# First group of a Strassen-like matmul: two sums of B ahead of a transpose, and the transfers of A and B interleaved

## The chip, the cores and the metric

One core of a Trainium2 chip. The time is the device time of one execution in microseconds (us); a median is over several executions of the same kernel. The span of a trace runs from the first to the last instruction of the traced execution and is some 1.6 us shorter than its time.

## The reference, cut to what matters

```python
def reference(a, b):            # a: 4096 x 4096, b: 4096 x 4096, float32
    x = np.matmul(a, b)
    return 0.5 * x * (1 + np.tanh(np.sqrt(2 / np.pi) * (x + 0.044715 * x**3)))
```

## The kernel before

The kernel computes each 2 x 2 block with seven products M1 to M7 instead of eight, on float16 copies of A and B that the loads cast from float32. A product's operands are blocks or sums of blocks: VectorE makes the sums ("aS" of A, "bS" of B) and transposes A. TensorE adds up a product's results in accumulators called banks. A block is 512 rows and the work goes in groups. Group 0 has nothing to hide its loads behind, so its first halves (suffix `_0` below) run as plain products and the second halves (`_1`) as M3, M5, M7, M1, M4, M2, M6. What each step waits for is put in a fixed order by hand.

```python
PRODUCTS = [                                   # name, bank, operand of A, operand of B
    ("M3", "Y", "11", ("12", "22", 1)),
    ("M5", "X", ("11", "12", -1), "22"),
    ("M7", "X", ("12", "22", -1), ("21", "22", 1)),
    ("M1", "X", ("11", "22", -1), ("11", "22", -1)),
    ("M4", "X", "22", ("21", "11", 1)),
    # ... M2, M6
]

def load_a(mb, quad, c, h=None):               # A: 4 transfers of 256 KB
    # ... cut
    for g in range(4):
        nc.gpsimd.dma_start(out=s[g * Q : (g + 1) * Q, x : x + n, :],
                            in_=a_v[kh * CH + c, g, :, x0 : x0 + n, :])

def make_sums(gi, s, q):                       # the sums of one step: A's, then B's
    # ... cut
    for tiles, blk, o, tag in ((a_tiles, mb, oa, "aS"), (b_tiles, nb, ob, "bS")):
        # ... cut
        t = pool.tile([P, 4 * NC], F16, name=tag, tag=tag, bufs=AHEAD + 1)
        nc.vector.tensor_tensor(out=t[:, :], in0=part(tiles, blk, o[0], q), in1=part(tiles, blk, o[1], q),
                                op=ALU.add if o[2] > 0 else ALU.subtract)

for n, whats in (                              # before step n: loads (A, B) and transposes (T)
    (0, "A11_0 B12_0 T11_0 B11_0 A12_0 B22_0 B21_0 A21_0"),
    (4, "T12_0 A22_0"),
    (7, "T21_0"),
    (8, "B12_1 B22_1 A11_1 T22_0 A12_1 B21_1"),
    (14, "T11_1 A22_1 B11_1"),
    (16, "T12_1 A21_1"),
    (18, "T22_1"),
    (22, "T21_1"),
): ...

for n, step in enumerate(steps):               # the order that every engine's queue gets
    for fn, args in before.get(n, ()):
        fn(*args)
    if n + AHEAD < len(steps):                 # sums two steps ahead
        make_sums(*steps[n + AHEAD])           # (cut: only for steps of products)
    flush()                                    # outputs that wait: add the plain part, Gelu, store
    combine()
    plain(n) if step[1] < 0 else multiply(*step)
```

M5's results are kept by ScalarE in buffers "m5" and go into outputs y; M7's results are copied by ScalarE out of their banks into buffers "x7", and M1 then adds into the same banks.

## Time and profile before

| | kernel before |
|---|---|
| median of three executions | 1582.06 us (1581.94 to 1584.08) |
| span in the trace (that execution took 1583.98 us) | 1582.3 us |
| TensorE busy | 1570.4 us |
| M5 ends, at full pace | 85.02 us |
| A22's second half transposed from | 82.89 us |
| M1 starts | 98.33 us |

TensorE is busy for 99% of the time, so the whole question is about 6.4 us between 85 and 98. The prediction below shows the lines for it. One more view belongs to it, GpSimd's timeline, as it issues the loads (start, duration, operation, how many, idle before):

```profile
55.33 0.65 POOL L149 DMA_DIRECT2D stage<-in_a_dram  x1 [0.36 <-issue]
57.52 4.46 POOL L149 DMA_DIRECT2D stage<-in_a_dram  x7 [1.54 <-issue]
```

The first line is the first transfer of A11, the second begins 1.54 us later: GpSimd stopped, and the trace names no semaphore for it.

### The profile page before, as it was taken

The numbers are of one execution on the slowest core, as the hardware profiler recorded it, in microseconds if no ns is written. First come the engines' busy times: TensorE is split into PE (matmuls) and PEld (weight loads), VectorE is DVE, ScalarE is ACT, GpSimd is POOL, SyncE is SP. The second block draws the span as 40 slices with busy tenths as digits, with TensorE's granted clock in tenths as the row PEclk, the third lists the DMA queues.
The fourth block names the chain that finished last, engine by engine and source line by source line (L and its number), as shares of the span: only waits on it lengthen the run. The fifth ranks groups of instructions, "written<-read, shape, count | busy, mean of one in ns | idle before, by whom it ended". The sixth has DMA issues, their size and how long they took to land. (4 is left out here: it accounts for less than half of the span.)

```text
span 1582.3 us, 19668 instructions
## 1 busy us (share of the span) xinstructions
PE 1570.4 (99%) x7254; PEld 710.5 (45%) x7254; DVE 1227.5 (78%) x1371; ACT 517.6 (33%) x710; POOL 535.7 (34%) x976
## 2 busy tenths in 40 slices
PE   9989999999999999999999999999999999999998
PEld 4434444444444444444444444444444444444443
DVE  1488898867877888895778788888687778988775
ACT  0026454411121545431112354542111145364111
POOL 7663441430333144341124414245011443314400
PEclk9999999999999999999999999999999999999999
DMA  9998793891957488587496837779468885748802
GB/s 174 188 221 182 107 191 68 152 184 31 204 97 146 110 133 160 104 161 135 72 168 115 183 76 137 150 109 191 81 115 151 134 160 90 150 107 133 161 27 81
DMA packets 224982, 211.12 MB, mean 133 GB/s; under 512 B 20080, under 2 KB 192112, under 8 KB 224880
## 3 DMA queue, kind: packets, MB, share of 16 engines
q0 software_dynamic: 187584, 142.67, 61.4%
q1 hardware_dynamic: 37296, 67.13, 11.8%
q8 instruction: 59, 0.97, 0.2%
q14 instruction: 43, 0.35, 0.1%
HBM read 285.22 MB, written 67.11 MB: 223 GB/s over the span
## 5 line engine op out<-in xcount | busy, mean ns | idle before, releaser
L310 PEld LDWEIGHTS <-aS 128*128 128x128 f16 x4960 | 485.6, 98 | 591.4 <-issue 4.4
L176 POOL DMA_DIRECT2D bR<-in_b_dram x832 | 447.8, 545 | 707.7 <-DVE bS L283 340.9
L283 DVE TENSOR_TENSOR aS<-aT 128x2048 f16<-128x2048 f16 x310 | 375.8, 1218 | 151.5 <-PE accX L310 115.0
L310 PE MATMUL accX<-bS,aS 128*128 128x512 f16 x1984 | 432.7, 380 | 4.5 <-DVE bS L283 2.5
L283 DVE TENSOR_TENSOR bS<-bR 128x2048 f16<-128x2048 f16 x310 | 375.8, 1217 | 69.4 <-PE accX L310 58.5
L310 PEld LDWEIGHTS <-aT 128*128 128x128 f16 x1984 | 194.1, 98 | 234.5 <-issue 0.5
L408 ACT ACTIVATE y<-y 128x512 f32<-128x512 f32 x192 | 118.5, 630 | 352.8 <-DVE y L417 352.4
L310 PE MATMUL accY<-bS,aT 128*128 128x512 f16 x992 | 216.9, 379 | 0.3 <-DVE bS L283 0.3
L310 PE MATMUL accY<-bS,aS 128*128 128x512 f16 x992 | 216.7, 379 | 0.0
L310 PE MATMUL accX<-bR,aS 128*128 128x512 f16 x992 | 216.7, 379 | 0.0
L310 PE MATMUL accX<-bS,aT 128*128 128x512 f16 x992 | 216.7, 379 | 0.0
L310 PE MATMUL accY<-bR,aS 128*128 128x512 f16 x992 | 216.7, 379 | 0.0
L149 POOL DMA_DIRECT2D stage<-in_a_dram x140 | 87.8, 633 | 247.8 <-DVE aT L162 176.5
L417 DVE TENSOR_TENSOR energy<-energy,square 128x1024 bf16<-128x1024 bf16 x240 | 164.2, 684 | 9.5 <-ACT square L200 5.7
L381 ACT COPY x<-accX 128x512 f32<-128x512 f32 x128 | 74.6, 585 | 223.7 <-PE accX L310 223.7
L200 ACT ACTIVATE square<-aT 128x1024 bf16<-128x1024 f16 x120 | 123.4, 1050 | 70.4 <-DVE energy L417 70.0
L200 ACT ACTIVATE square<-bR 128x1024 bf16<-128x1024 f16 x120 | 123.0, 1050 | 62.4 <-DVE energy L417 60.5
L162 DVE STREAM_TRANSPOSE aT<-stage 128x2048 uint32<-128x2048 uint32 (+1 forms) x36 | 74.3, 2067 | 66.0 <-DMA stage<-in_a_dram 66.0
L381 ACT COPY m<-accX 128x512 f32<-128x512 f32 x60 | 34.8, 580 | 198.6 <-PE accX L310 192.1
L408 ACT ACTIVATE y<-accX 128x512 f32<-128x512 f32 x64 | 38.2, 597 | 100.2 <-PE accX L310 99.9
L417 DVE TENSOR_TENSOR x<-accX,x 128x512 f32<-128x512 f32 x64 | 44.0, 691 | 21.9 <-ACT y L408 19.1
L417 DVE TENSOR_TENSOR y<-accY,m 128x512 f32<-128x512 f32 x60 | 39.9, 686 | 12.5 <-ACT m L381 12.4
(40 smaller groups left out, 341.2 us busy)
## 6 DMA issues: line engine op xcount, KB each, us to landing
bR<-in_b_dram POOLq DMA_DIRECT2D x832, 128.0 KB, 5.2
out_dram<-y SPq DMA_DIRECT2D x256, 256.0 KB, 5.8
stage<-in_a_dram POOLq DMA_DIRECT2D x116, 256.0 KB, 6.8
stage<-in_a_dram POOLq DMA_DIRECT2D x24, 128.0 KB, 5.1
row<-seen_d SPq DMA_DIRECT2D x2, 1.5 KB, 3.8
seen_d<-seen SPq DMA_DIRECT2D x1, 3.0 KB, 7.1
```

Of the source, the lines that this page charges most:

```text
L149: nc.gpsimd.dma_start(out=s[g * Q : (g + 1) * Q, x : x + n, :], in_=a_v[kh * CH + c, g, :, x0 : x0 + n, :],)
L162: nc.vector.transpose(dst[:, :, x, :], src[:, :, x, :])
L176: nc.gpsimd.dma_start(out=t[g * Q : (g + 1) * Q, e::2, :], in_=b_v[kh * CH + c, g, e, :, :, n0 : n0 + NC],)
L200: nc.scalar.activation(t[:, :], src, ACT.Square)
L283: nc.vector.tensor_tensor(out=t[:, :], in0=part(tiles, blk, o[0], q), in1=part(tiles, blk, o[1], q), op=ALU.add if o[2] > 0 else ALU.subtract,
L310: nc.tensor.matmul(acc[:, :], sa[:, j // 2, i * P : (i + 1) * P, j % 2], sb[:, j, :], start=start and j == 0, stop=stop and j == 3, skip_g ...
L381: nc.scalar.copy(out=t[:, :], in_=src[:, :])
L408: nc.scalar.activation(y[:, :], src[:, :], ACT.Gelu_apprx_tanh)
L417: nc.vector.tensor_tensor(out=o[:, :], in0=x[:, :], in1=y[:, :], op=op)
```

## The change

The intent is twofold. M7's two sums of B need no transpose, so they can be made while VectorE waits for A22. And A's transfers are twice as large as B's, so interleaving them keeps more bytes in flight, as only eight transfers are ever under way (in the trace each issue waits for the landing of the eighth one back). The core of the diff:

```diff
-        for g in range(4):
-            nc.gpsimd.dma_start(out=s[...], in_=a_v[...])
+        return [(s[...], a_v[...]) for g in range(4)]
...
+    def load(*pairs):
+        lists = [fn(*args) for fn, args in pairs]
+        order = sorted(((k + 0.5) / len(ts), x, k) for x, ts in enumerate(lists) for k in range(len(ts)))
+        for _, x, k in order:
+            dst, src = lists[x][k]
+            nc.gpsimd.dma_start(out=dst, in_=src)
...
-    def make_sums(gi, s, q):
+    def make_sums(gi, s, q, only=None):        # only="bS": B's sum now, kept for the step
...
-        (8, "B12_1 B22_1 A11_1 T22_0 A12_1 B21_1"),
+        (8, "A11_1+B12_1+B22_1 T22_0 A12_1+B21_1"),
...
-        (18, "T22_1"),
+        (18, "S2 S3 T22_1"),
```

`S2 S3` are the two sums of B for M7's two steps; `+` joins loads that are interleaved. The other groups' loads go through `load` one at a time, in their old order.

More of the change, by code (lines that the diff above doesn't have):

```diff
@@ L147, in load_a @@
         s = staged[mb, quad, c]
-        for g in range(4):
-            nc.gpsimd.dma_start(
-                out=s[g * Q : (g + 1) * Q, x : x + n, :],
-                in_=a_v[kh * CH + c, g, :, x0 : x0 + n, :],
-            )
+        return [
+            (s[g * Q : (g + 1) * Q, x : x + n, :], a_v[kh * CH + c, g, :, x0 : x0 + n, :])
+            for g in range(4)
+        ]
     def turn_a(mb, quad, c, h=None):
@@ L173, in load_b @@
         t = b_tiles[nb, quad, c]
-        for e in range(2) if h is None else (h,):
-            for g in range(4):
-                nc.gpsimd.dma_start(
-                    out=t[g * Q : (g + 1) * Q, e::2, :],
-                    in_=b_v[kh * CH + c, g, e, :, :, n0 : n0 + NC],
-                )
+        return [
+            (t[g * Q : (g + 1) * Q, e::2, :], b_v[kh * CH + c, g, e, :, :, n0 : n0 + NC])
+            for e in (range(2) if h is None else (h,)) for g in range(4)
+        ]
+    def load(*pairs):
+        lists = [fn(*args) for fn, args in pairs]
+        order = sorted(
+            ((k + 0.5) / len(ts), x, k) for x, ts in enumerate(lists) for k in range(len(ts))
+        )
+        for _, x, k in order:
+            dst, src = lists[x][k]
+            nc.gpsimd.dma_start(out=dst, in_=src)
     def part(tiles, blk, quad, q):
@@ L278, in make_sums @@
         for tiles, blk, o, tag in ((a_tiles, mb, oa, "aS"), (b_tiles, nb, ob, "bS")):
+            if only not in (None, tag):
+                continue
             if isinstance(o, str):
                 got.append(part(tiles, blk, o, q))
+                continue
+            if (tag, gi, s, q) in sums:
+                got.append(sums.pop((tag, gi, s, q)))
                 continue
@@ L287, in make_sums @@
             got.append(t)
+            if tag == only:
+                sums[tag, gi, s, q] = t
+                return
         sums[gi, s, q] = got
@@ L480, in half_path @@
         for what in whats.split():
-            fn = {"A": load_a, "B": load_b, "T": turn_a}[what[0]]
-            for h in (0, 1) if what[4] == "0" and what != "A11_0" else (None,):
-                before.setdefault(n, []).append((fn, (0, what[1:3], int(what[4]), h)))
+            half = what[-1] == "0" and what != "A11_0"
+            if what[0] == "S":
+                before.setdefault(n, []).append((make_sums, (0, 2, int(what[1]), "bS")))
+                continue
+            for h in (0, 1) if half else (None,):
+                args = [(x[0], (0, x[1:3], int(x[4]), h)) for x in what.split("+")]
+                if what[0] == "T":
+                    before.setdefault(n, []).append((turn_a, args[0][1]))
+                else:
+                    pairs = [({"A": load_a, "B": load_b}[x], xs) for x, xs in args]
+                    before.setdefault(n, []).append((load, pairs))
     before[4].append((idle, (N_IDLE,)))
@@ L504, in half_path @@
                 early = gi == 0 and c == 0
-                at(gi, 3 - early, 2 * c + 1, load_b, nb1, "12", c)
-                at(gi, 4 - early, 2 * c + 1, load_b, nb1, "22", c)
-                at(gi, 6, 2 * c + 1, load_b, nb1, "21", c)
+                at(gi, 3 - early, 2 * c + 1, load, (load_b, (nb1, "12", c)))
+                at(gi, 4 - early, 2 * c + 1, load, (load_b, (nb1, "22", c)))
+                at(gi, 6, 2 * c + 1, load, (load_b, (nb1, "21", c)))
             if na:
-                at(gi, 4, c, load_a, mb1, "11", c)
+                at(gi, 4, c, load, (load_a, (mb1, "11", c)))
                 at(gi, 5, 2 * c, turn_a, mb1, "11", c)
-                at(gi, 5, 2 * c + 1, load_a, mb1, "12", c)
+                at(gi, 5, 2 * c + 1, load, (load_a, (mb1, "12", c)))
                 at(gi, 6, 2 * c, turn_a, mb1, "12", c)
-                at(gi, 6, 2 * c + 1, load_a, mb1, "22", c)
+                at(gi, 6, 2 * c + 1, load, (load_a, (mb1, "22", c)))
                 at(gi + 1, 0, 2 * c + 1, turn_a, mb1, "22", c)
-                at(gi + 1, 1, c, load_a, mb1, "21", c)
+                at(gi + 1, 1, c, load, (load_a, (mb1, "21", c)))
                 at(gi + 1, 3 + c, 0, turn_a, mb1, "21", c)
             if nbb:
-                at(gi, 6, 2 * c + 1, load_b, nb1, "11", c)
+                at(gi, 6, 2 * c + 1, load, (load_b, (nb1, "11", c)))
     for mb in range(NMB):
```

## The prediction

> **What bounds the kernel now.** First the page: the engine rows and the slices say which engine sets the end.
>
> ```profile
> span 1582.3 us, 19668 instructions
> PE 1570.4 (99%) x7254; PEld 710.5 (45%) x7254; DVE 1227.5 (78%) x1371; ACT 517.6 (33%) x710; POOL 535.7 (34%) x976
> PE   9989999999999999999999999999999999999998
> ```
>
> TensorE is idle for 1582.3 - 1570.4 = 11.9 us in all. About 1.4 us lie before the first matmul and about 5 us behind the last one (the final output), so no reordering in the first group can win more than some 6 us, 0.4% of the time. The third slice is one of the few below 9, so next I read the list of TensorE's waits:
>
> ```profile
> PE accX L310 <- DVE bS L283: 2.5, 1, 2.5
> PE accX L310 <- DVE aS L283: 1.6, 1, 1.6
> PE accX L310 <- ACT m L381: 0.4, 1, 0.4
> ```
>
> Then TensorE's own timeline around them (start, duration, operation, count, idle before):
>
> ```profile
> 87.66 3.13 PE L310 MATMUL accX<-bS,aS 128*128 128x512 f16 x8 [2.48 <-DVE bS L283]
> 91.20 5.52 PE L310 MATMUL accX<-bS,aS 128*128 128x512 f16 x24 [0.41 <-ACT m L381]
> 98.33 7.07 PE L310 MATMUL accX<-bS,aS 128*128 128x512 f16 x32 [1.62 <-DVE aS L283]
> ```
>
> The first two rows are M7 of group 0 (32 matmuls), the third is M1. M5 ended at 85.02 in issue time (78.11 + 32 x 0.216). At full pace M7 would run from 85.02 and M1 from 91.93; M1 starts at 98.33. So **6.4 us** are lost here, and M4, M2 and everything later follow from M1's start almost without a wait. The start of M1 is therefore the quantity to predict. Its cause is on VectorE, which works its queue in order:
>
> ```profile
> 82.89 2.31 DVE L162 STREAM_TRANSPOSE aT<-stage 128x2048 uint32<-128x2048 uint32 x1 [4.90 <-DMA stage<-in_a_dram]
> 85.24 1.23 DVE L283 TENSOR_TENSOR aS<-aT 128x2048 f16<-128x2048 f16 x1
> 86.38 1.22 DVE L283 TENSOR_TENSOR bS<-bR 128x2048 f16<-128x2048 f16 x1
> 87.52 1.22 DVE L283 TENSOR_TENSOR aS<-aT 128x2048 f16<-128x2048 f16 x1
> 88.65 1.22 DVE L283 TENSOR_TENSOR bS<-bR 128x2048 f16<-128x2048 f16 x1
> 89.79 2.68 DVE L417 TENSOR_TENSOR y<-accY,m 128x512 f32<-128x512 f32 x4
> 92.39 1.21 DVE L283 TENSOR_TENSOR aS<-aT 128x2048 f16<-128x2048 f16 x1
> 93.52 1.22 DVE L283 TENSOR_TENSOR bS<-bR 128x2048 f16<-128x2048 f16 x1
> 94.65 2.49 DVE L417 TENSOR_TENSOR y<-y,x 128x512 f32<-128x512 f32 x4
> 97.71 2.03 ACT L381 COPY x<-accX 128x512 f32<-128x512 f32 x4
> ```
>
> VectorE sits idle for 4.90 us until A22's second half lands, transposes it, and from there to 97 has no gap at all. The last line is ScalarE's: the copies of M7's banks, which M1 overwrites. They stand behind four Gelus, which wait for the additions at 94.65. First copy 97.71 + 0.58 = 98.29, M1 at 98.33: M1 waits for this chain, and "aS" in its wait row is only the tie that ended last by name. So M1 = start of A22's transpose (82.89) + 15.44 us of serial work.
>
> **What the Trainium skill says.** "VectorE: DVE Perf Modes", section "The perf-mode tier table": a 16-bit tensor_tensor of 2048 elements takes 1224 ns at the 2x rate. The trace agrees: 1218 ns, with 1.13 to 1.14 us from start to start. "DMA: Bandwidth & Descriptors", section "Where 436 GB/s comes from": about 358 GB/s from HBM and 435 GB/s of fabric per core. These loads cast float32 to half, so they read twice what they write; the trace's best stretches write 202 GB/s, thus read 404: between the two figures, and I take the DMA engines as the bound of the loads rather than the number of bytes in flight. "TensorE: Matmul & The Clock Gate", section "What's actually happening": activity is judged in free-running windows of 3413 ns, and an idle one halves the clock. The trace has one such window, after the 2.48 us of idle time:
>
> ```profile
> 84.00:88.00 4.00, 1.52 (x8) 0.55 (x7) 3.96 (x4) 0.08 (x1) 3.94 (x7) 1.00 1.27 188
> 88.00:92.00 4.00, 3.59 (x11) 1.16 (x9) 3.89 (x6) 1.17 (x2) 1.81 (x4) 0.57 1.43 193
> 96.00:100.00 4.00, 2.38 (x12) 0.98 (x11) 4.00 (x5) 3.74 (x8) 2.80 (x7) 1.00 1.21 230
> ```
>
> The granted clock (third number from the end) falls to 0.57 there: M7's first eight matmuls take 3.13 us instead of 1.7. After the 1.62 us of idle time it stays at 1.00. So a window need not be wholly idle to be punished, but 1.6 us of 3.4 are not enough.
>
> **The change, part 1: M7's two sums of B go in front of A22's transpose.** Nothing is added or removed; two tensor_tensors move. They need B21 and B22 only. B21 lands at about 77 in the kernel before (its eight issues start between 62 and 72 and land some 5 us after the last), so they fit in the 4.90 us where VectorE waits. Behind the transpose 2 x 1.135 = 2.27 us fall away. M1 = transpose + 15.44 - 2.27 = transpose + **13.17 us**.
>
> **Part 2: transfers woven.** In the changed order the 16 issues of B12 and B22 take A11's four in between (B B A B B ...), and B21's eight take A12's four (B A B B A B ...); A22 follows alone as before. Bytes ahead of A22 are the same. What the kernel before loses there is seen in GpSimd's issues: it stops 1.54 us between A11's first and second issue, for no semaphore that the trace names and while VectorE is idle; an issue always starts about 0.3 us after the landing of the eighth one back, so only eight transfers are in flight, and eight of B (128 KB each) are just 5.2 us of work at 0.65 us each. So a stop empties the engines:
>
> ```profile
> 52.00:56.00 4.00, 4.00 (x20) 1.86 (x19) 0.00 (x0) 1.30 (x3) 3.19 (x6) 1.00 1.24 202
> 60.00:64.00 4.00, 4.00 (x20) 1.85 (x19) 0.00 (x0) 0.00 (x0) 2.65 (x6) 1.00 1.31 168
> 72.00:76.00 4.00, 4.00 (x21) 1.81 (x19) 3.97 (x5) 0.00 (x0) 3.65 (x7) 1.00 1.15 173
> ```
>
> From the landings one by one: 2.92 us between A11's first two where 1.32 is the pace (1.6 lost), and about 0.6 lost over A22's own four, when only B's were in flight ahead of them: 2.2 us at most to be had. With A woven in, eight issues hold 1.6 of A's on average in the first stretch and 2.7 in the second, which is 6.3 and 7.0 us of work instead of 5.2. I expect the 0.6 back and 0.4 of the 1.6, as the stop stays. A22 would land at 82.8 - 1.0 = 81.8.
>
> But weaving makes **A12 later**. It landed whole at 71.67, with B21 behind it; now its last piece is the eleventh of twelve. From 48.94 (the landing before this stretch) come 24 issues of B at 0.65 and 8 of A at 1.32 = 26.2 us, so B21 is done at 75.1 without any stop and A12 at 74.5; with 1.2 us of stop, at 75.7. Its transpose started at 73.30 and now starts at about 75.8; M5 needs it plus the first difference, 2.33 + 1.2 us, thus 79.3 instead of 78.11: **a new wait of about 1.2 us before M5** (0 without any stop). VectorE then goes on: transpose 2.33, four sums at 1.135, so it comes to A22's transpose at 75.8 + 2.33 + 4.54 = **82.7**. A22 has landed by then; the order on VectorE, not the transfer, sets it.
>
> **Sum.** M1 = 82.7 + 13.2 = 95.9 instead of 98.33: 2.4 us sooner. M5's wait and M7's disappear in it: M7 starts at 82.7 + 2.33 + 1.2 = 86.2, close behind M5's end (79.3 + 6.9), waits some 0.7 us for its third bank (ScalarE's copy behind the first y), ends near 93.9, and M1 waits some 2 us for its copies. Behind M1 the order is the old one, and the later loads have slack or move with the rest. 1582.06 - 2.4 = **1579.6**.
>
> **Rivals.** (1) The stop disappears too, since more is in flight: A12 at 74.5, A22's transpose at 81.4, M1 at 94.6, time 1578.3. For it: the deeper stock of work; against: GpSimd issues nothing in that time whatever the order. (2) The wait moves to A12: if it lands at 77, M5 waits 2.5 us, VectorE comes to A22's transpose at 84, M1 at 97, and 1581 remain. For it: M5's margin before was 1.3 us only (its first difference done at 76.8, used at 78.11). (3) The idle time before M1 (1.6 us before, about 2 now) may fall into one clock window and cost up to 1.7 us at half rate on the very chain that sets the end: 1581.3. For it: 2.48 us did it; against: 1.62 did not. One chance in four; where the window lies differs between executions, which may also be why the three runs before spread over 2.1 us. (4) The full 6.4 us come back: 1575.7; against it stands the chain of y, Gelu and copies, which the change leaves.
>
> **Range and chances.** Rivals 1 and 2, with about 0.5 us of spread between runs, give 1577.6 to 1581.6. A 2% step is 31.6 us, five times all that TensorE loses in this place; nothing that the change touches could add that much either, as the instructions are the same. Faster by over 2%: 0.004; within 2%: 0.99; slower: 0.006.
>
> **What would show it.** In VectorE's timeline: two bS between the second aS of M5 and A22's transpose, the transpose at 82 to 83 with little or no idle time before it, M1 some 13.2 us later. In TensorE's: a new wait of 0 to 1.5 us before M5 (near 78), under 0.5 before M7, about 2 before M1. In the rates: no stretch near 170 GB/s around A22's issues. It is wrong if A22's transpose still waits for its transfer, if M1 follows the transpose by 15 us, if the half clock falls on M1, or if the gain is lost later to a wait for outputs in group 1.

## The result, and the profile after

| | before | changed |
|---|---|---|
| median of six executions | 1582.88 us (1581.94 to 1584.08) | 1580.62 us (1579.66 to 1581.45) |
| ratio | | 0.9985 (95%: 0.9972 to 0.9998) |
| span in the trace | 1582.3 | 1578.4 |
| A22's transpose | 82.89 | 81.35 |
| M1 starts | 98.33 | 94.52 |

A ratio is from runs of both kernels in the same rounds; it isn't quite the ratio of the medians or of the means. The gain is 2.3 us by medians, where 2.4 were forecast, and 1580.62 lies in the range.

TensorE's timeline of the changed kernel in the same place (M7 in two rows, then M1):

```profile
85.34 1.89 PE L325 MATMUL accX<-bS,aS 128*128 128x512 f16 x8
87.39 5.34 PE L325 MATMUL accX<-bS,aS 128*128 128x512 f16 x24 [0.16 <-ACT m L396]
94.52 7.07 PE L325 MATMUL accX<-bS,aS 128*128 128x512 f16 x32 [1.79 <-ACT x L396]
```

The wait before M7 is gone, the one before M1 has stayed (1.79 us against 1.62) and in this trace carries the name of ScalarE's copy, where the trace of before had put "aS" (the two end within 0.01 us of each other there; e5 below tells them apart). With the waiting gone, the half clock in M7 (the stretch with a granted clock of about half) is gone too: its first eight matmuls take 1.89 us, not 3.13. VectorE's timeline (M1's two sums at 88.57 and 89.71 left out), and after it the line of ScalarE's copies:

```profile
74.46 2.31 DVE L161 STREAM_TRANSPOSE aT<-stage 128x2048 uint32<-128x2048 uint32 x1 [2.05 <-DMA stage<-in_a_dram]
76.81 2.36 DVE L295 TENSOR_TENSOR aS<-aT 128x2048 f16<-128x2048 f16 x2
79.08 2.35 DVE L295 TENSOR_TENSOR bS<-bR 128x2048 f16<-128x2048 f16 x2
81.35 2.30 DVE L161 STREAM_TRANSPOSE aT<-stage 128x2048 uint32<-128x2048 uint32 x1
83.69 2.36 DVE L295 TENSOR_TENSOR aS<-aT 128x2048 f16<-128x2048 f16 x2
85.97 2.69 DVE L432 TENSOR_TENSOR y<-accY,m 128x512 f32<-128x512 f32 x4
90.84 2.49 DVE L432 TENSOR_TENSOR y<-y,x 128x512 f32<-128x512 f32 x4
```

```profile
93.90 2.03 ACT L396 COPY x<-accX 128x512 f32<-128x512 f32 x4
```

The two bS now stand ahead of A22's transpose, which starts without any idle time: from 74.46 on, VectorE has no gap. The idle time has gone to A12's transpose instead (2.05 us), which begins 1.2 us later than before. The rates (last number, GB/s) in the stretches in which the kernel before fell to 168 and 173:

```profile
60.00:64.00 4.00, 4.00 (x21) 1.77 (x19) 0.62 (x1) 0.00 (x0) 2.94 (x6) 1.00 1.31 197
72.00:76.00 4.00, 4.00 (x20) 1.82 (x19) 1.95 (x2) 0.00 (x0) 2.82 (x5) 1.00 1.40 197
```

One thing doesn't fit yet: the pair of traces shows 3.9 us (spans) or 3.8 us (M1), the medians 2.3. The experiments take that up too.

### The profile page after: what moved, and what is told of

It is laid out like the page before. It is cut to its first block, busy times and chain, and to the rows that moved or that the text cites. A ratio compares the mean times of both kernels' runs of the same rounds, so it can differ in the third digit from the quotient of the medians. Undisturbed runs are those within 1.5% of the kernel's fastest.

```text
span 1578.4 us, 19668 instructions
## 1 busy us (share of the span) xinstructions
PE 1568.0 (99%) x7254; PEld 710.0 (45%) x7254; DVE 1228.0 (78%) x1371; ACT 517.8 (33%) x710; POOL 537.4 (34%) x976
## 5 line engine op out<-in xcount | busy, mean ns | idle before, releaser
L161 DVE STREAM_TRANSPOSE aT<-stage 128x2048 uint32<-128x2048 uint32 (+1 forms) x36 | 74.4, 2068 | 62.5 <-DMA stage<-in_a_dram 49.0
```

The costliest lines, as they stand in the source:

```text
L161: nc.vector.transpose(dst[:, :, x, :], src[:, :, x, :])
```

## The experiments

My theory: M1's start sets the time, and it follows the start of A22's transpose by a fixed stretch of VectorE's and ScalarE's work, 15.4 us in the old order and 13.2 in the new; the transpose starts at A22's landing or when VectorE comes to it, whichever is later. Rivals: only the transfers count; or only the order does; or the rest of the gain was lost to the half clock. All twelve runs gave correct results, and each ran in five rounds beside the kernel before. There were three sets of rounds, e1 to e4, e5 to e8 and e9 to e12; "the same rounds" means one set, and the second set has no run of the changed kernel. A time given first is the median of its runs, with the ratio to the kernel before and its 95% interval behind it. Where an interval includes 1, as for e2, e4, e7 and e12, the time alone shows no difference from the kernel before.

### The sums alone (e1, e12) and the weaving alone (e2)

```diff
 e1, e12 (from the changed kernel)
-        (8, "A11_1+B12_1+B22_1 T22_0 A12_1+B21_1"),
+        (8, "B12_1 B22_1 A11_1 T22_0 A12_1 B21_1"),
 e2 (from the changed kernel)
-        (18, "S2 S3 T22_1"),
+        (18, "T22_1"),
```

> Only the two sums of B are moved; the transfers stay in the old order. Chain theory: A22's transpose again starts when its transfer lands (82.9 us, as in the kernel before, with 2.5 us or so of VectorE idle time ahead of it), and M1 follows it by 13.2 us, so M1 starts near 96.1 and the time is 2.3 us under before. Rival (only the earlier landing of A22 counts, the sums lie beside other work): M1 stays near 98.3 and the time within 0.5 us of before. GpSimd's stop falls on A11's issues again and leaves a rate near 170 GB/s.

> Only the transfers are woven; the sums stay behind A22's transpose. Chain theory: A12 lands near 74.4 and its transpose and M5's two sums end near 79.2; A22's transpose then waits for its landing (80.4), starts near 80.5, and M1 follows by 15.4 us: 95.9, time 2.4 us under before. So each part alone gives over half of the trace's 3.8 us and together they give less than their sum (4.7). Rival (the woven transfers are worth nothing without the moved sums, or everything): 0 or 3.8 us.

> The sums alone moved, transfers in the old order, a second time, beside the changed kernel. Its first run stood 0.85 us above the changed kernel in the same rounds, though its M1 came as early (94.4), because of a wait at 1187 us for a late transfer in another group. Theory (the weaving is worth little when A22 lands at 80.5 to 81 and something when it lands late): the mean is 0 to 1 us above the changed kernel, and this trace's M1 is A22's transpose + 13.2 again, 94.4 to 96. Rival (the weaving is worth its 2.4 us): 2 us above.

Measured: the sums alone 1580.48 (ratio 0.9983, 0.9970 to 0.9997) and, on the second occasion, 1581.38 (0.9989, 0.9976 to 1.0003); the weaving alone 1581.22 (0.9990, 0.9977 to 1.0004). In means of the same rounds that is 2.4, 2.2 and 1.4 us under before. M1 started at 94.39, 94.11 and 95.70 us. The forecast for e1 had the right 13.2 us and too late a transpose: with the transfers in the old order it started at 81.22, not 82.9.

```profile
81.22 2.31 DVE L161 STREAM_TRANSPOSE aT<-stage 128x2048 uint32<-128x2048 uint32 x1 [2.46 <-DMA stage<-in_a_dram]
```

So VectorE does wait for A22 there, as expected, but the transpose starts 1.7 us earlier than in the first trace of before, in the same order of transfers: A22's last piece landed at 80.67, there at 82.77. Landings differ that much between executions. (In e1 and e12 the transpose starts 0.55 us after the landing, in the other traces that wait for it 0.12 to 0.13; why stays open.) e2 came out as forecast in the trace (transpose 80.26, M1 95.70), and smaller in the times.

### The two kernels again (e3, e8, e11)

> The changed kernel once more, for a second trace and five more times. The first trace shows M1 3.8 us sooner, the medians only 2.3 us. Theory: the difference is spread at the start of the run (how soon the first loads of A11 land, which moves all that follows by about 1 us) and not a cost of the change; then the interval between A12's landing and M1 is again 20.1 us in this trace while the start of the first real matmul differs, and the mean gain over all rounds comes out between 2.3 and 3.8. Rival: in some executions the half clock falls on M1 (idle 1.8 us before it), then this trace may show eight or more matmuls of M1 at 427 ns, and the times fall in two clumps 1.5 us apart.

> The kernel before once more, for a second trace. Theory: M1 follows A22's transpose by 15.4 us in this trace too, whatever A22's landing; where A22 lands differs between executions (80.7 in the run with the sums alone moved, 82.8 in the first trace of before, with the same order of transfers), so M1 lies between 96.1 and 98.4. If A22 lands near 81 here as well, the first trace of the kernel before was an unlucky one and the gain of the change is nearer 2.3 us than 3.8. Rival: A22 lands at 82.8 again and M1 starts at 98.3.

> The changed kernel a third time, on the same chip as the two before and the one after, so that they are compared in the same rounds. Theory: M1 at 94.5, mean 2.3 to 3.2 us under the kernel before.

Measured: the changed kernel 1579.51 (ratio 0.9979, 0.9965 to 0.9993) and 1580.96 (0.9985, 0.9971 to 0.9999), means 3.2 and 2.5 us under before; the kernel before against itself 1582.44 (1.0003, 0.9990 to 1.0017). In e8 A22's transpose on VectorE and M1 on TensorE read:

```profile
80.60 2.31 DVE L162 STREAM_TRANSPOSE aT<-stage 128x2048 uint32<-128x2048 uint32 x1 [4.20 <-DMA stage<-in_a_dram]
```

```profile
96.04 7.07 PE L310 MATMUL accX<-bS,aS 128*128 128x512 f16 x32 [1.80 <-ACT x L381]
```

The kernel before is here 2.3 us earlier at both places than in its first trace, and the distance is again 15.44 us. The first trace had been an unlucky one: its execution took 1583.98 us, 1.9 us above the median of the three runs then known. That clears up the 3.8 against 2.3 us: averaged over the traces of each kernel, M1 starts at 97.2 us before ((98.33 + 96.04) / 2) and at 94.9 after ((94.52 + 94.57 + 95.52) / 3), which is 2.3 us. (Means of two and three traces are coarse; that they meet the medians so closely is in part luck.) The rival of the half clock falls: none of the three traces of the changed kernel shows a slow matmul in M1 after its 1.8 us of idle time. Ten traces, those of before, of the changed kernel and of e1, e2, e6, e7 and e12, in one table (us; "idle" is VectorE's before A22's transpose):

| trace | idle | A22's transpose | M1 | distance | span | span - M1 |
|---|---|---|---|---|---|---|
| before | 4.90 | 82.89 | 98.33 | 15.44 | 1582.3 | 1484.0 |
| before, again (e8) | 4.20 | 80.60 | 96.04 | 15.44 | 1580.9 | 1484.9 |
| weaving alone (e2) | 1.31 | 80.26 | 95.70 | 15.44 | 1580.4 | 1484.7 |
| sums alone (e1) | 2.46 | 81.22 | 94.39 | 13.17 | 1580.0 | 1485.6 |
| sums alone (e12) | 2.02 | 80.94 | 94.11 | 13.17 | 1578.4 | 1484.3 |
| changed | 0 | 81.35 | 94.52 | 13.17 | 1578.4 | 1483.9 |
| changed (e3) | 0 | 81.40 | 94.57 | 13.17 | 1578.5 | 1483.9 |
| changed (e11) | 0 | 82.35 | 95.52 | 13.17 | 1579.6 | 1484.1 |
| A12 first (e6) | 2.83 | 81.53 | 94.70 | 13.17 | 1579.2 | 1484.5 |
| A in halves (e7) | 0 | 82.52 | 95.69 | 13.17 | 1579.8 | 1484.1 |

The distance is the same to 0.01 us wherever the order is the same. The span is M1 plus 1483.9 to 1485.6 us; what it varies by is mostly a wait in a much later group, which comes in some executions of any version and not in others, in e1 for instance

```profile
1187.35 2.97 PE L325 MATMUL accY<-bS,aT 128*128 128x512 f16 x13 [1.14 <-DVE bS L295]
```

because a transposed block of A landed late there. (e8 shows 0.67 us, e6 0.39 and e2 0.23 at the same spot.) So e1's trace has the second earliest M1 in the table and not the second shortest span.

What each part is worth together with the other: the changed kernel is 0.85 us under the sums alone in the rounds of e3 and e1, and 0.3 us in those of e11 and e12, with 0.4 to 0.7 us of spread between runs. The weaving adds something between nothing and 1 us to the moved sums; these rounds don't settle it closer. So the moved sums are most of the gain.

### Bytes in flight or order (e7), and A12's place (e6)

```diff
 e7: A11 and A12 go in two halves of 128 KB, in the same woven order
+                if "+" in what:
+                    args = [(args[0][0], (*args[0][1][:3], k)) for k in (0, 1)] + args[1:]
 e6: A12 ahead of B21, A11 still woven
-        (8, "A11_1+B12_1+B22_1 T22_0 A12_1+B21_1"),
+        (8, "A11_1+B12_1+B22_1 T22_0 A12_1 B21_1"),
```

> The changed kernel, woven in the same order of bytes, but A11 and A12 go in pieces of 128 KB, so that eight transfers in flight are 1.0 MB as in the kernel before. Theory (weaving helps because eight issues hold more bytes, which covers GpSimd's stop of 1.5 us): the stop shows in the landings again (1 to 1.6 us lost), A12 lands near 75.5, A22's transpose starts near 82.4, M1 near 95.6, 1 us later than in the changed kernel. Rival (order alone matters): A22's transpose at 81.4 and M1 at 94.5 as in the changed kernel.

> The changed kernel, with A12's four transfers in front of B21's eight again (A11 stays woven). Bytes ahead of A22 are the same. Theory (in the changed kernel A12's late landing and the order on VectorE set the start of A22's transpose, not A22's own landing): A12 lands near 70, M5's sums are done by 76, VectorE idles for 1 to 2 us again ahead of A22's transpose, which starts at A22's landing, 80.4 to 81, and M1 starts 13.2 us later, 93.6 to 94.2: 0.4 to 0.9 us sooner than the changed kernel. Rival (A22's landing sets it already): no change, or later if A22 lands later because eight B's are in flight ahead of it (82, M1 at 95).

e7 measured 1581.41 (ratio 0.9993, 0.9980 to 1.0007), 1.8 us above e6 in the same rounds by means. A22's transpose started at 82.52 and M1 at 95.69, as the theory had said (82.4 and 95.6). GpSimd's stop and the rate right after it:

```profile
56.00 2.16 POOL L186 DMA_DIRECT2D bR<-in_b_dram  x4 [1.85 <-issue]
```

```profile
60.00:64.00 4.00, 4.00 (x21) 1.79 (x19) 0.00 (x0) 0.00 (x0) 2.79 (x6) 1.00 1.18 155
```

The changed kernel stops as well:

```profile
55.22 2.16 POOL L186 DMA_DIRECT2D bR<-in_b_dram  x4 [1.40 <-issue]
```

and yet its rate stays at 197. The order of bytes is the same in both; eight transfers in flight are 1.0 MB in the one, some 1.2 MB in the other. That speaks for the stock in flight, as the change intended, and against the order alone. One pair of stretches would be thin, but the landings of all kept traces agree. From the landing before this stretch to A22's last one, the same bytes took 32.2 to 33.8 us in the old order (before, e8, e1, e12), 31.6 to 32.3 in the eight traces woven as in the changed kernel, and 33.5 in e7. The stop is not always hidden: from 60 to 64 us the rate was 196 to 199 in six of the eight, but 187 in e11 and 190 in e10. (e7 has eight issues more than the changed kernel; this run doesn't separate that from their size.)

e6 measured 1579.49 (0.9980, 0.9966 to 0.9994), M1 at 94.70, no earlier than in two of the three traces of the changed kernel, so the number expected of it was missed (its set of rounds has no run of the changed kernel to compare times with). Half of the theory held: with A12 early, VectorE idled again (2.83 us), so A22's landing set its transpose. But A22 landed later, as the rival had it (33.4 us on the count above): the transpose started at 81.53. In the changed kernel the two limits, A12 followed by VectorE's own work and A22's landing, lie within about 1 us of each other, so that pushing one uncovers the other.

### The wait that is left before M1 (e4, e5)

```diff
 e4 (from the changed kernel)
-            flush()
+            if step[:2] != (0, 2):              # not during M7
+                flush()
 e5 (from the changed kernel): the additions at once, Gelu and store at M1
-            flush()
+            flush(step[:2] != (0, 2))
```

> The changed kernel, with the additions and Gelus of M5's four outputs put off to M1's first step, so that ScalarE copies M7's banks as soon as M7 leaves them. Chain theory (M1 waits for ScalarE's copies behind the Gelus): the 1.8 us of idle time before M1 vanish, M1 starts near 92.7, time 1.8 us under the changed kernel, about 1578.8. Rival (M1 waits for its sums on VectorE, as the wait row of the kernel before said): M1 stays near 94.5 and the time at 1580.6.

> The failed run before this one showed M1 waiting 5.1 us for ScalarE's copies, because a copy's buffer is the one that the addition behind M5 reads, and the additions had been put off. Here the additions stay where they are and only the four Gelus are put off to M1's first step. Theory (the copies need the buffers that the additions free, and then stand behind the Gelus): the first addition ends near 91.5, the copies run from there, M1 starts near 92.6 without the 1.8 us of idle time, time 1.8 us under the changed kernel. Rival (the additions alone hold the copies, the Gelus cost nothing): M1 stays at 94.5.

e4 failed: 1585.03 (1.0011, 0.9998 to 1.0025), 5.1 us above e3 in the same rounds by means.

```profile
97.06 9.78 PE L325 MATMUL accX<-bS,aS 128*128 128x512 f16 x32 [5.09 <-ACT x L396]
```

M1 waited 5.09 us, and the half clock then took 2.7 us more from it (9.78 us for 32 matmuls, elsewhere 7.07). The copies of M7 need the buffers that hold the plain products' part, and these are free only when `flush` has added it to y. I had overlooked that. e5 keeps the additions and puts off only the Gelus: 1580.08 (0.9982, 0.9969 to 0.9996). M7 and M1 now run as one, M1 at 92.4 us (85.49 + 32 x 0.216), 2.1 us sooner than in the changed kernel, as the theory had it: M1 had waited for ScalarE's copies behind the Gelus. The time did not follow (2.7 us under before, where the changed kernel had 2.3 to 3.2):

```profile
85.49 14.07 PE L325 MATMUL accX<-bS,aS 128*128 128x512 f16 x64
115.14 7.07 PE L325 MATMUL accY<-bS,aS 128*128 128x512 f16 x32 [1.77 <-DVE y L434]
```

M6 waits until VectorE has read M2's results. VectorE works from 74.4 to 122 us without a gap, so M6 cannot start before about 115.1, and the changed kernel's M6 starts at 115.24 without a wait that the list shows:

```profile
115.24 7.07 PE L325 MATMUL accY<-bS,aS 128*128 128x512 f16 x32
```

M1's wait and VectorE's order hide each other.

### Both limits at once (e9, e10)

```diff
 e10 (from the changed kernel); e9 is this together with e5
+            late = step == (0, 5, 3)            # M2's last step: read its results first,
-                if s >= 0:
+                if s >= 0 and not late:
                     make_sums(gi, s, q)
...
                 multiply(*step)
+            if late:                            # then make the sums of M6's second half
+                make_sums(gi, s, q)
...
         elif name == "M6":
-            y = new_y()
+            y = new_y() if gi or i in (0, 3) else pool.tile([P, NC], F32, name="m5", tag="m5", bufs=2)
```

> The run with only the Gelus put off won M1's 1.8 us and lost 1.77 us again before M6, which waits for VectorE to read M2's results. VectorE works without a gap from A12's transpose (74.4) to 122, so this is its own order. Here, beside the late Gelus, M2's four y go in front of the sums for M6's second half (2.27 us sooner), and two of M6's outputs use the idle m5 buffers so that they do not wait for output transfers. Theory (VectorE's order between A22's transpose and M6 is what is left): M1 near 92.5, M6 near 113.2 to 113.6 instead of 115.2, the first step of group 1's second half near 127.3 instead of 129.4, time 1.7 to 2.1 us under the changed kernel. Rival (the wait moves once more, to outputs or to group 1's sums): time as the changed kernel.

> As the run before, but the Gelus of M5 stay where the changed kernel has them. Theory (two waits that hide each other): M1 starts at 94.5 as in the changed kernel, so M6 cannot start before 115.2 whatever VectorE does, and nothing is won: within 0.4 us of the changed kernel. Rival: the order of the y is worth its 2 us by itself.

e9 measured **1578.09** (1577.44 to 1578.69; ratio to before 0.9969, 0.9955 to 0.9983). It beats both kernels: by means 5.3 us under before and 2.8 us under the changed kernel of the same rounds (e11), more than the 1.7 to 2.1 us forecast. In the trace M6 starts at 112.71 without a wait before it, and group 1's second half at 126.96:

```profile
112.71 7.18 PE L325 MATMUL accY<-bS,aS 128*128 128x512 f16 x32
126.96 7.07 PE L325 MATMUL accY<-bS,aT 128*128 128x512 f16 x32 [0.17 <-DVE bS L295]
```

The changed kernel has 129.40 for the latter. e10 measured 1579.47 (0.9976, 0.9962 to 0.9989). Its trace has M1 at 94.67 and M6 at 115.38, so nothing was won up to there, as expected; by means it is yet 1.5 us under e11, where at most 0.4 had been expected. Part of that is the wait of 0.2 to 0.5 us before group 1's second half, which the three traces of the changed kernel have and e10 lacks; part is that e11's trace ran 0.9 us behind e10's even before M3. The rest stays open. The edit also does two things at once: the order of VectorE's work, and two outputs of M6 in the buffers "m5". In e10's trace VectorE waits 1.49 us for an output transfer behind M6, against 2.56 to 2.81 in the changed kernel; no run separates the two. So the traces show the two limits up to M6, but the times don't show that neither part gains alone: e10 has 1.5 of e9's 2.8 us.

## Why the prediction was right

- **M1 sets the time.** Right. In ten traces the span is M1 plus 1483.9 to 1485.6 us.
- **15.44 us of serial work, less 2.27 for the two sums: 13.17.** Right to the last digit, in both orders and in every trace.
- **VectorE's order, not A22's landing, sets the transpose.** Right: no idle time ahead of it in three traces of the changed kernel.
- **The transpose at 82.7, against 82.89 before.** Mis-sized at both ends. It came at 81.35, 81.40 and 82.35; the term that failed is the stop of GpSimd, of which I gave back 0.4 of 1.6 us. It was covered wholly in the first trace (197 GB/s where before had 168), so A12 landed at about 74.4 and not at 75.7: rival 1. And 82.89 was itself the late end of before; the second trace had 80.60. The two errors are of nearly one size and cancel: averaged over the traces the transpose starts at 81.75 us before and at 81.70 after, 0.05 us sooner, where 0.2 was forecast. That the two errors cancel was luck. What the 2.4 us rest on is the other term, the 2.27 us of the moved sums, and that was right.
- **A new wait of 1.2 us before M5.** It followed from the same term and was not there (0 to 0.1 us in the three traces of the changed kernel). e7, in which the stop is not covered, has it: 1.11 us.
- **M7's third bank 0.7 us, M1's copies about 2 us.** 0.16 and 1.79 in the first trace; right in kind.
- **The half clock on M1, one chance in four.** It did not come after 1.8 us of idle time; it did come after 5.09 (e4).
- **1579.6 against 1580.62.** Of the 1.0 us, 0.8 is the start of the sum: the three runs then known of the kernel before had a median of 1582.06, all six have 1582.88. The sum also took a saving read from the trace of a slow execution (1583.98 us) off that median. So rival 1's M1 (94.6) came true in the first trace, but not its time (1578.3).
- **Not seen:** that the copies also need buffers which the additions free (e4), and that VectorE, with no gap from A12's transpose on, holds M6 at the same moment at which M1's wait releases it (e5). The prediction gave only the chain of y, Gelu and copies as the reason why the full 6.4 us would not come back; with that chain cut, VectorE's order gave nothing back either.

## What to carry to other kernels

When a nearly full engine waits, find the serial stretch that ends in the wait and count it: here 15.44 and 13.17 us came back in every trace, while the starting point moved by 2 us between executions, so take a second trace before believing a difference of that size. Work that needs no late transfer belongs ahead of the transfer's wait, and a fixed number of transfers in flight holds more bytes when large ones stand among the small ones. When a wait that was removed does not shorten the time, look for a second limit that ends at the same moment.

## What the Trainium skill lacked or had wrong

- "TensorE: Matmul & The Clock Gate", section "What's actually happening", calls the clock halved after at least one idle window of about 3.4 us. Here 2.48 us of idle time, less than one window, were followed by a stretch with a granted clock of 0.57, while some 1.8 us before M1 were not in any of ten traces that had them; after 5.09 us M1 took 9.78 us instead of 7.07. In the first trace the half clock lasted 3.41 us (88.17 to 91.59 us). Counting windows of that length from each trace's own changes of clock, 2.48 and 3.41 us idle within one window were followed by the half clock, and up to 1.80 us were not.
- "DMA: Bandwidth & Descriptors", section "SWDGE vs HWDGE vs iDMA", names VectorE's two-port modes as what locks GpSimd out of the memory that its rings stand in. In every trace of this case GpSimd stopped issuing for 1.4 to 1.85 us while VectorE was idle, with no semaphore named, always close to the same amount of issued work: ahead of A11's second transfer in the old order, some four transfers sooner in the woven one. What it waits for stays open.
- The same page, section "Measured (HBM→SBUF, 128 partitions, SWDGE, issued from GpSimd)", has no rate for loads that cast. Here float32 to half reached 202 GB/s written.
